# RWKV scan: the joins of the next inverse issued ahead of the scan step, in a PSUM bank of their own, with the inverse and the norms at other places of the step

## The chip, the core and the metric

The kernel runs on one core of a Trainium2 chip. The metric is the device time of one execution in microseconds (us): the median over the runs, each timed from start to end. A profile of one more execution shows each engine by itself: PE (TensorE matmuls; PEld is its weight loads), DVE (VectorE), ACT (ScalarE), POOL (GpSimd) and SP (SyncE, which issues the DMAs). Each engine runs its own list of instructions in the order in which the built program holds them; an instruction whose data or buffer isn't ready holds up those behind it on its engine.

## What is computed

A two-layer backbone over 1024 latent tokens and 256 context tokens of width 1024. Each layer mixes tokens by four groups of heads (mLSTM, Hyena, retention, RWKV-7), projects their outputs together, and ends in a convolutional feed-forward network. The change is in the RWKV group. Its scan, over four heads of 64 channels and in both directions, is

```
def step(s_mem, inp):
    rt, wt, kt, vt, at, bt = inp
    sa = jnp.einsum('bhvk,bhk->bhv', s_mem, at)
    s_new = s_mem * wt[:, :, None, :] + sa[..., None] * bt[:, :, None, :] + vt[..., None] * kt[:, :, None, :]
    return s_new, jnp.einsum('bhvk,bhk->bhv', s_new, rt)
```

followed by `out = g * (head_group_norm(h) + bonus)`. The mLSTM group runs over the same tokens at the same time and shares no data with RWKV until the output projection `y @ w_out`.

## The kernel before

The scan is done in ten steps of 128 tokens, one tile for the forward direction and one for the backward one; each tile holds two chunks of 64 tokens. A step has four parts, each a function:

- `rwkv_prep(s)` loads the step's inputs, makes decays and scaled keys (two gate projections on PE at L496, then ACT and DVE), and forms the 64x64 products of a chunk (`G`, PE at L533) and transposed keys (`bt`, L544). It needs nothing of the scan.
- `rwkv_inverse(s)` inverts the 16x16 diagonal blocks of each chunk's triangular matrix: one DVE transpose into `LM` (L555) and thirty dependent POOL instructions on `XL` (L559, L560).
- `rwkv_tail(s)` joins these blocks into the 64x64 inverse `XT`: two joins (16 to 32, 32 to 64), each of small 32*32 matmuls (L576, L584, L585, L590, L597, L598, L605, L606) with DVE or ACT copies between them. L569 is its first instruction, L611 its last.
- `rwkv_chain(s)` is the scan step itself: for each of two chunks and two directions it multiplies the state (L631, L632), copies (`U`, L634), applies `XT` (L635), copies (`VSA`), and makes the new state (L641, L642, then L644 on DVE); L649 and L650 make the outputs `y`. Step s needs the state of step s-1 and `XT` of step s.

`group_norm` then normalises tiles that both directions have finished (steps 1 and 6 to 9), through a scratch tile `gq`, and stores them (`yw<-gq`).

The PSUM (eight banks) is cut for this stage by `psum(k,cbank=2,ybank=1,pbank=1,dbank=2,mbank=2)`: `cbank` for the scan step and the joins, `pbank` for the gate projections, `dbank` for the products of `rwkv_prep`, `ybank` for outputs, `mbank` for mLSTM and the ada steps.

`layer` starts the scan, issues its first steps, and then `mlstm`, which calls back: 19 side steps in the first layer (17 in the second), each with a share of the modulation matrix (the ada steps, L993) and every second one with a step of the scan. The mLSTM first walks the chunks (states, L753 and L759), then makes ten (eight) tiles of output (L781, L791, L797, L804). The order in which a function is called is only a priority: a scheduler in the build sets each engine's final order from it. After the scan, `load_wo` brings in the output weights (32 loads `wst<-in_w_out`, each split by ACT and DVE at L1035 and L1036), and `mix_out` gathers normalised tiles (`yt<-ym,yh,yr,yw`), transposes them (L1166), splits them (`uh`, L1177) and multiplies (L1042 to L1044). The weights `wo` take memory that the mLSTM held, `yt` takes memory that includes pool `p3` of the scan, and `uh` takes that of the scan's other pools.

Of the kernel before, what the change touches and what calls it, by code (L numbers as in the profile page):

```python
# [10 lines left out]
F32=mybir.dt.float32  # L11
# [418 lines left out]
def rwkv(K,l,pv,last,p1,p2,p3):  # L430


    nc=K.nc; tt=nc.vector.tensor_tensor
    YF=p1.tile([128,10,4,64],F32,name="YF")
    W2=p1.tile([128,512],F32,name="W2"); nc.gpsimd.memset(W2,0.0)
    for i,(w,o) in enumerate((('rwkv_w2','rwkv_w0'),('rwkv_a2','rwkv_a0'))):
        nc.sync.dma_start(W2[i*64:i*64+32].rearrange("p (d c) -> p d c",d=2),K.a[w][l].rearrange("d p c -> p d c"))
        nc.sync.dma_start(W2[i*64+32:i*64+33],K.a[o][l:l+1].rearrange("o d c -> o (d c)"))
    TWA=p1.tile([128,2,2,128],F32,name="TWA"); nc.gpsimd.memset(TWA,0.0)
    rmask=p1.tile([128,2,128],F32,name="rmask"); nc.sync.dma_start(rmask,K.a['c_rwmask'])  # L440
    xl0=p1.tile([128,32,8],F32,name="xl0"); nc.sync.dma_start(xl0,K.a['c_xl0'])
    smask=p1.tile([128,4*65],F32,name="smask"); nc.gpsimd.memset(smask,1.0); nc.gpsimd.memset(smask.rearrange("p (a b) -> p a b",b=65)[:,:,0:1],0.0)
    kas=p1.tile([128,2,2,2],F32,name="kas")
    for a in range(2):
        r=slice(64,128) if a==0 else slice(0,64); o=slice(0,64) if a==0 else slice(64,128)
        nc.gpsimd.memset(kas[o,a],-0.5)
        nc.vector.tensor_scalar(out=kas[r,a,0],in0=pv['ka'][r],scalar1=0.5,scalar2=None,op0=ALU.mult)
        nc.vector.tensor_scalar(out=kas[r,a,1],in0=pv['ka'][r],scalar1=-0.5,scalar2=1.0,op0=ALU.mult,op1=ALU.add)
    AR=[p1.tile([128,2,2,2,2,2,64],F32,name="AR%d"%i) for i in range(3)]
    for t in AR: nc.gpsimd.memset(t[64:128,:,:,:,0],0.0); nc.gpsimd.memset(t[0:64,:,:,:,1],0.0)  # L450
    XT=[p1.tile([128,2,4,128],F32,name="XT%d"%i) for i in range(2)]
    for t in XT: nc.gpsimd.memset(t,0.0)
    I32=p1.tile([128,32],F32,name="I32"); hm=p1.tile([128,2],F32,name="hm"); PI=p1.tile([128,2,4,32],F32,name="PI")
    for i in range(4): nc.scalar.activation(out=I32[i*32:i*32+32],in_=K.ident[i*32:i*32+32,i*32:i*32+32],func=ACTF.Copy)
    for i in range(2): nc.vector.tensor_reduce(out=hm[:,i:i+1],in_=I32[:,i*16:i*16+16],axis=XS,op=ALU.add)
    for i in range(2): nc.scalar.activation(out=PI[:,i],in_=I32.unsqueeze(1).to_broadcast([128,4,32]),func=ACTF.Copy)
    C=dict(AR=AR,XT=XT,I32=I32,hm=hm,PI=PI,YF=YF,W2=W2,TWA=TWA,rmask=rmask,xl0=xl0,smask=smask,kas=kas,p=p2,p3=p3,l=l,pv=pv,last=last,seen=set())
    NS=10
    st=[rwkv_prep(K,C,0)]
    rwkv_inverse(K,C,st[0]); rwkv_tail(K,C,st[0])  # L460
    st.append(rwkv_prep(K,C,1))
    for s in range(NS):
        yield
        if s+1<NS: rwkv_inverse(K,C,st[s+1])
        rwkv_chain(K,C,st[s],st[s+1] if s+1<NS else None,s)
        if s==1 and not last or s>5:
            a,b={1:(8,9),6:(3,4),7:(2,5),8:(1,6),9:(0,7)}[s]
            sl=slice(a,b+1,b-a)
            group_norm(K,YF[:,sl],K.D['yw'].rearrange("(t p) c -> p t c",p=128)[:,sl],2,p2.tile([128,1056],F32,tag="LM",name="gq")[:,0:512].rearrange("p (a t) -> p a t",t=64),"gnw")
        if s+1<NS: rwkv_tail(K,C,st[s+1])  # L470
        if s+2<NS: st.append(rwkv_prep(K,C,s+2))


def rwkv_prep(K,C,s):
    nc=K.nc; act=nc.scalar.activation; tt=nc.vector.tensor_tensor; mm=nc.tensor.matmul; ts=nc.vector.tensor_scalar
    p=C['p']; p3=C['p3']; pv=C['pv']; bank=K.dbank; A=ALU
# [12 lines left out]
    VSA,SV=[X.rearrange("p q d c f e -> p d c q f e") for X in (VSA,SV)]  # L489
    lw=p3.tile([128,8,65],F32,tag="lw",name="lw"); As=p3.tile([128,2,2,128],F32,tag="As",name="As")  # L490
    act(out=lw[:,:,0:1],in_=C['rmask'][:,0,0:1].unsqueeze(1).to_broadcast([128,8,1]),func=ACTF.Copy,scale=0.0)
    bb=[K.pbank(),K.pbank()]
    for i in range(2):
        for d in range(2):
            for ft in range(2):
# [26 lines left out]
    for d in range(2):  # L522
# [8 lines left out]
        for c in range(2):  # L531
            b=bank()
# [8 lines left out]
        b=bank()  # L541
# [21 lines left out]
def rwkv_tail(K,C,P):  # L563
# [5 lines left out]
    for h in range(2): nc.vector.transpose(out=T2[:,4*h:4*h+4].rearrange("p j k d u -> p j (k d u)"),in_=X[:,h*128:h*128+128].rearrange("p (i j) -> p j i",j=4))  # L569
    nc.vector.transpose(out=DT,in_=T2.rearrange("p j k d u -> p (d u) (j k)"))  # L570
    R=[(q,blk,slice(q*64+blk*32,q*64+blk*32+32)) for q in range(2) for blk in range(2)]
    b=K.cbank()
    for d in range(2):
        for u in range(4):
            c,f=u//2,u%2; o=slice(d*64+u*16,d*64+u*16+16)
# [1 line left out]
    for d in range(2):  # L577
        o=slice(d*16,d*16+16)
        nc.vector.scalar_tensor_tensor(out=PI[:,d,:,o],in0=b[:,d*64:d*64+64].rearrange("p (u t) -> p u t",t=16),scalar=C['hm'][:,1-d:2-d],in1=C['I32'][:,o].unsqueeze(1).to_broadcast([128,4,16]),op0=A.mult,op1=A.add)
    b=K.cbank(); Q=p.tile([128,4,32],F32,tag="Q",name="Q"); ZC=p.tile([128,4,32],F32,tag="AX",name="ZC")  # L580
    for u in range(4):
        o=slice(256+u*32,288+u*32)
        for q,blk,r in R:
# [5 lines left out]
            o=slice(d*128+u*32,d*128+u*32+32)  # L589
            for q,blk,r in R: mm(b[r,o],PI[r,d,u],T2[r,:,:,1,u] if d else DT[r,u],start=True,stop=True)  # L590
    for q,blk,r in R: act(out=XT[r,:,:,r],in_=b[r,0:256].rearrange("p (d u t) -> p d u t",d=2,u=4),func=ACTF.Copy)
    b=K.cbank()
    for u in range(4):
        c,f=u//2,u%2; o=slice(u*32,u*32+32)
        for q in range(2):
# [1 line left out]
            mm(b[hi,o],G[lo,0,c,f,q,32:64],ZC[lo,u],start=True,stop=True)  # L597
            mm(b[lo,o],G[hi,1,c,f,q,0:32],ZC[hi,u],start=True,stop=True)  # L598
    act(out=Q.rearrange("p u t -> p (u t)"),in_=b[:,0:128],func=ACTF.Copy)
    b=K.cbank()  # L600
    for u in range(4):
        o=slice(u*32,u*32+32)
        for q in range(2):
# [769 lines left out]
def layer(k,l,out):  # L1373
    nc=k.nc; last=l==1
    D=k.D=k.Ds[l]; k.Dn=k.Ds[l+1] if not last else None
    with ExitStack() as es:
# [19 lines left out]
            with k.tc.tile_pool(name="rt",bufs=1,side="right") as k.p_rt:  # L1396
                retention(k,l,last)
        close_u(k)
        psum(k,cbank=2,ybank=1,pbank=1,dbank=2,mbank=2)
        with ExitStack() as ew:  # L1400
            with ExitStack() as er:
                R=lambda **kw: er.enter_context(k.tc.tile_pool(bufs=1,side="right",**kw))
# [66 lines left out]
```

## Time and profile before

| what | us |
|---|---|
| median of 3 runs | 4250.28 |
| lowest and highest run | 4240.55, 4259.92 |
| the profiled execution, its own time | 4248.15 |
| span of its instructions | 4246.4 |

The RWKV scan and the mLSTM run together twice, once in each layer: from about 767 to 1234 us and from 2942 to 3369 us of the span. The rest (projections, Hyena, retention, feed-forward) isn't touched. Busy time is the time in which an engine had at least one instruction under way; a matmul counts from its start to the end that the profile models, so two matmuls that overlap count once. Times of rows are microseconds from the start of the span, unless marked ns. Two records of PE stand for one fp32 matmul of the program.

### The profile page before, as it was taken

To read this page: it belongs to the slowest core of one execution; us is meant where nothing else is said; L and a number is where in the kernel's file an instruction comes from. 1 tells how busy PE (TensorE), PEld (TensorE's weight loads), DVE (VectorE), ACT (ScalarE), POOL (GpSimd) and SP (SyncE) were. 2 spreads that over 40 slices of the span, in tenths; PEclk is the share of its full clock that TensorE was granted. 3 is DMA by queue.
4 is the path that set the end of the run, shared out by engine and by line. 5 is a ranking of instruction groups with operands and counts; after the bars stand their busy time and mean duration, and the time that the engine had idled before them with its cause. 6 is when DMAs were issued, how large, how long until landed. Compare 5 with 4: busy or idle time off the path is not lost.

```text
span 4246.4 us, 70484 instructions
## 1 busy us (share of the span) xinstructions
PE 3951.2 (93%) x28176; PEld 3225.0 (76%) x28176; DVE 2537.2 (60%) x4756; ACT 1413.6 (33%) x2849; POOL 764.7 (18%) x1538
## 2 busy tenths in 40 slices
PE   5999999799979999999997999997899799999998
PEld 2788887677768888888885678886776678888886
DVE  5755665777669444444448565677767684444447
ACT  4433333554344211111113433344543442212121
POOL 3320023323312000000021221025432220000002
PEclk6999999799989999999998999998898799999999
DMA  4235554344443110111103325554333331111112
GB/s 165 76 96 180 151 156 121 109 149 125 129 147 120 46 40 30 45 40 35 35 30 121 90 87 157 171 162 118 118 115 109 124 111 55 50 40 55 45 50 99
DMA packets 477154, 414.50 MB, mean 98 GB/s; under 512 B 48827, under 2 KB 443284, under 8 KB 474010
## 3 DMA queue, kind: packets, MB, share of 16 engines
q1 hardware_dynamic: 476826, 409.99, 31.1%
q8 instruction: 222, 3.64, 0.3%
q14 instruction: 106, 0.87, 0.1%
HBM read 323.65 MB, written 86.25 MB: 97 GB/s over the span
## 4 chain that ended last, share of the span: by engine, by line
PE 53%; DVE 9%; DMA 4%; issue 2%; ACT 2%; POOL 1%; SPq 1%; DVEq 0%; ACTq 0%; POOLq 0%
PE bank L1043 9%; PE bank L1042 9%; PE bank L1044 9%; PE dbank L1042 6%; PE dbank L1043 6%; PE dbank L1044 6%; DVE bst L1003 1%; DMA xt<-x 1%; DVE facc L1225 1%; PE mbank L993 1%; PE bank L186 1%; DMA adaw<-in_ada_w 1%; PE bank L187 1%; DVE facc L1226 0%; DMA wst<-in_w_out 0%
## 5 line engine op out<-in xcount | busy, mean ns | idle before, releaser
L1042 PE MATMUL dbank<-uh,wh 128*128 128x512 f32 (+1 forms) x2120 | 763.7, 369 | 8.6 <-ACT tmpB L398 5.5
L1043 PE MATMUL dbank<-ul,wh 128*128 128x512 f32 (+1 forms) x2120 | 759.8, 367 | 0.0
L1036 DVE TENSOR_TENSOR wl<-wst,wh 128x1024 fp32r<-128x1024 f32 x146 | 185.9, 1275 | 510.3 <-ACT wh L1035 355.1
L1044 PE MATMUL dbank<-uh,wl 128*128 128x512 f32 (+1 forms) x2120 | 481.5, 367 | 0.0
L1042 PEld LDWEIGHTS dbank<-uh,wh 128*128 128x128 f32 x2120 | 400.6, 189 | 84.0 <-ACT tmpB L398 5.9
L1043 PEld LDWEIGHTS dbank<-ul,wh 128*128 128x128 f32 x2120 | 400.9, 189 | 68.7 <-issue 1.1
L1044 PEld LDWEIGHTS dbank<-uh,wl 128*128 128x128 f32 x2120 | 365.7, 188 | 71.0 <-issue 1.7
L1284 DVE TENSOR_TENSOR facc<-facc,bank 128x512 f32<-128x512 f32 x324 | 221.8, 687 | 205.1 <-PE bank L1044 205.1
L1042 PE MATMUL bank<-uh,wh 128*128 128x512 f32 (+1 forms) x920 | 334.9, 372 | 4.5 <-ACT uh L1030 4.5
L1043 PE MATMUL bank<-ul,wh 128*128 128x512 f32 (+1 forms) x920 | 335.1, 372 | 0.8 <-DVE ul L1031 0.8
L1042 PE MATMUL bank<-wdh,gh 128*128 128x512 f32 x792 | 315.6, 400 | 15.7 <-DVE facc L1298 5.7
L1043 PE MATMUL bank<-wdl,gh 128*128 128x512 f32 x792 | 310.4, 392 | 1.0 <-DVE wdl L1036 1.0
L1253 POOL MEMSET fz<- 128x1 f32 x132 | 7.3, 99 | 1433.4 <-DVE fc L1268 1213.5
L1044 PE MATMUL bank<-wdh,gl 128*128 128x512 f32 x792 | 247.7, 391 | 0.0
L1035 ACT ACTIVATE wh<-wst 128x1024 fp32r<-128x1024 f32 x146 | 154.7, 1060 | 237.5 <-PE dbank L1043 164.5
L1035 ACT ACTIVATE wdh<-wst 128x1024 fp32r<-128x1024 f32 x46 | 48.8, 1062 | 523.7 <-PE bank L1044 431.4
L1044 PE MATMUL bank<-uh,wl 128*128 128x512 f32 (+1 forms) x920 | 211.9, 372 | 0.0
L1042 PEld LDWEIGHTS bank<-uh,wh 128*128 128x128 f32 x920 | 174.1, 190 | 36.1 <-ACT uh L1030 5.6
L1043 PEld LDWEIGHTS bank<-ul,wh 128*128 128x128 f32 x920 | 174.2, 189 | 31.9 <-DVE ul L1031 1.7
L1042 PEld LDWEIGHTS bank<-wdh,gh 128*128 128x128 f32 x792 | 149.7, 189 | 56.9 <-DVE facc L1298 11.0
L1044 PEld LDWEIGHTS bank<-uh,wl 128*128 128x128 f32 x920 | 161.5, 188 | 33.1
L1043 PEld LDWEIGHTS bank<-wdl,gh 128*128 128x128 f32 x792 | 149.7, 189 | 34.6 <-issue 3.2
(490 smaller groups left out, 7856.9 us busy)
## 6 DMA issues: line engine op xcount, KB each, us to landing
wst<-in_ffn_w_up SPq DMA_DIRECT2D x88, 512.0 KB
adaw<-in_ada_w SPq DMA_DIRECT2D x160, 256.0 KB
wst<-in_w_in SPq DMA_DIRECT2D x58, 512.0 KB
wst<-in_ffn_w_down SPq DMA_DIRECT2D x46, 512.0 KB
df<-in_c_F SPq DMA_DIRECT2D x10, 1344.0 KB
xt<-x SPq DMA_DIRECT2D x26, 512.0 KB
df<-in_c_I SPq DMA_DIRECT2D x8, 1344.0 KB
rkk<-wrk SPq DMA_DIRECT2D x10, 1024.0 KB
```

The costliest lines, as they stand in the source:

```text
L186: mm(dst_re,F[:,i],pre(slot),start=True,stop=False); mm(dst_re,F[:,i+1],pim(slot),start=False,stop=True)
L187: mm(dst_im,F[:,i],qim(slot),start=True,stop=False); mm(dst_im,F[:,i+2],qre(slot),start=False,stop=True)
L993: for j in range(2): nc.tensor.matmul(ps[32*j:32*j+2,0:128],k.sc[:,q],w[u][q//2][:,q%2,j*128:j*128+128],start=(q==0),stop=(q==7))
L1003: for h in range(2): nc.vector.bn_stats(out=st[:,h],in_=x[h])
L1035: k.nc.scalar.activation(out=h,in_=st,func=ACTF.Copy)
L1036: k.nc.vector.tensor_tensor(out=lo,in0=st,in1=h,op=ALU.subtract)
L1042: mm(ps,lh,rh,start=(i==0),stop=False)
L1043: mm(ps,lh,rl,start=False,stop=False)
L1044: for i,((lh,ll),(rh,rl)) in enumerate(pairs): mm(ps,ll,rh,start=False,stop=(i==n-1 and more is None))
L1225: for o,i,gg in zip([y[:,h] for h in hs],x,[g[:,h] for h in hs]) if parts else [(y,x,g)]: stt(out=o,in0=i,scalar=m,in1=gg,op0=ALU.subtract ...
L1253: for q in (0,1025,1282): nc.gpsimd.memset(z[:,q:q+1],0.0)
L1284: else: tt(out=d,in0=d,in1=ps,op=ALU.add)
```

## The change

The call of `rwkv_tail` for step s+1 moves ahead of `rwkv_chain` for step s; `rwkv_prep` for step s+2 moves directly behind the scan step, with `rwkv_inverse` for step s+2 right after it (before, that was called at the start of the next round); `group_norm` comes last in the round. The joins take their PSUM from a bank of their own, `tbank`; `pbank` is given up and the gate projections use `dbank`. The scratch tile of the norm moves from the buffer of `LM` (pool `p2`) to that of `As` (pool `p3`).

```diff
-    st.append(rwkv_prep(K,C,1))
+    st.append(rwkv_prep(K,C,1)); rwkv_inverse(K,C,st[1])
     for s in range(NS):
         yield
-        if s+1<NS: rwkv_inverse(K,C,st[s+1])
+        if s+1<NS: rwkv_tail(K,C,st[s+1])
         rwkv_chain(K,C,st[s],st[s+1] if s+1<NS else None,s)
+        if s+2<NS: st.append(rwkv_prep(K,C,s+2)); rwkv_inverse(K,C,st[s+2])
         if s==1 and not last or s>5:
             a,b={1:(8,9),6:(3,4),7:(2,5),8:(1,6),9:(0,7)}[s]
             sl=slice(a,b+1,b-a)
-            group_norm(K,YF[:,sl],K.D['yw'].rearrange("(t p) c -> p t c",p=128)[:,sl],2,p2.tile([128,1056],F32,tag="LM",name="gq")[:,0:512].rearrange("p (a t) -> p a t",t=64),"gnw")
-        if s+1<NS: rwkv_tail(K,C,st[s+1])
-        if s+2<NS: st.append(rwkv_prep(K,C,s+2))
+            group_norm(K,YF[:,sl],K.D['yw'].rearrange("(t p) c -> p t c",p=128)[:,sl],2,p3.tile([128,8,64],F32,tag="As",name="gq"),"gnw")
...
-    bb=[K.pbank(),K.pbank()]
+    bb=[bank(),bank()]
...
-    b=K.cbank()
+    b=K.tbank()
...
-        psum(k,cbank=2,ybank=1,pbank=1,dbank=2,mbank=2)
+        psum(k,cbank=2,tbank=1,ybank=1,dbank=2,mbank=2)
```

The third edit stands at all four places of `rwkv_tail` that take a bank. From `rwkv_prep` on, the changed kernel's line numbers are one lower.

How the instructions stand on PE in the middle of the first layer, at the end of a scan step that the joins for the next one follow (`T` and `DT` are the transposed blocks, `mCS` and `mq` belong to the mLSTM). Before:

```order
L642 MATMUL cbank<-VSA,bt 64x64 x2
L649 MATMUL ybank<-VSA,G 64x64
L650 MATMUL ybank<-SV,AR_6744 64x64 x2
L649 MATMUL ybank<-VSA,G 64x64 x2
L650 MATMUL ybank<-SV,AR_6744 64x64 x2
L649 MATMUL ybank<-VSA,G 64x64 x2
L650 MATMUL ybank<-SV,AR_6744 64x64 x2
L576 MATMUL cbank<-T_11506,G 32x16 x16
L576 MATMUL cbank<-DT,G 32x16 x16
L797 MATMUL mbank<-mCS,mq_10058 128x130 x2
```

The joins begin when the scan step's last output matmul has been issued. In the changed kernel, inside a scan step of the same layer (L589 and L596 are joins, L634, L640 and L641 the scan step, L803 the mLSTM):

```order
L634 MATMUL cbank<-U,XT_6752 128x64 x2
L589 MATMUL tbank<-DT,PI 32x32 x13
L780 MATMUL mbank<-mRU,mVOr 128x512
...
L589 MATMUL tbank<-DT,PI 32x32 x3
L589 MATMUL tbank<-T_10755,PI 32x32 x11
L803 MATMUL mbank<-mV,S 128x65 x4
L589 MATMUL tbank<-T_10755,PI 32x32 x5
L640 MATMUL cbank<-SV,ident 64x64 x2
L641 MATMUL cbank<-VSA,bt 64x64 x2
```

The joins of the next step stand between the scan step's own matmuls, and in shorter pieces. At the end of the second layer, PE has before (L804 is the last mLSTM matmul, the rest of the scan step follows it):

```order
L804 MATMUL mbank<-mV,S 128x65 x4
L635 MATMUL cbank<-U,XT_25742 128x64 x2
L804 MATMUL mbank<-mV,S 128x65 x4
L631 MATMUL cbank<-SV,G 64x64 x2
L632 MATMUL cbank<-SV,AR_25735 64x64 x2
```

Behind these rows come the rest of scan step 8, the joins for step 9, all of scan step 9, and L1042. Now, at the same place:

```order
L631 MATMUL cbank<-SV,AR_25733 64x64 x2
L803 MATMUL mbank<-mV,S 128x65 x8
L634 MATMUL cbank<-U,XT_25743 128x64 x4
L648 MATMUL ybank<-VSA,G 64x64 x2
L649 MATMUL ybank<-SV,AR_25733 64x64 x2
```

Only the last product and the outputs of scan step 9 stand behind the last mLSTM matmul. On SP, at the end of the same layer, before:

```order
L1158 DMA yt<-ym_108 128x2x256
L1158 DMA yt<-yh_109 128x2x256
L1158 DMA yt<-yr_110 128x2x256
L1158 DMA yt<-yw_111 128x2x256
L679 DMA ym_108<-gq 128x2x256
L1060 DMA wst<-in_w_out 128x256 x22
L679 DMA yw_111<-gq 128x2x256
```

and now:

```order
L678 DMA ym_108<-gq 128x2x256
L678 DMA yw_111<-gq 128x2x256
L1059 DMA wst<-in_w_out 128x256 x24
L1157 DMA yt<-ym_108 128x2x256
L1157 DMA yt<-yh_109 128x2x256
L1157 DMA yt<-yr_110 128x2x256
L1157 DMA yt<-yw_111 128x2x256
```

The second layer's first gathers for the output projection stand behind all loads of its weights, where two sets of them stood ahead. In the first layer two sets stand ahead of the 24 loads in both kernels.

## Rows read from the trace of the kernel before

**Rows 1.** The page, busy time of PE.

```profile
PE 3951.2 (93%) x28176; PEld 3225.0 (76%) x28176; DVE 2537.2 (60%) x4756; ACT 1413.6 (33%) x2849; POOL 764.7 (18%) x1538
```

**Rows 2.** Windows: length, busy PE, PEld, DVE, ACT, POOL, clock, DMA share, GB/s.

```profile
850.00:1185.00 335.00, 314.56 (x5462) 239.03 (x5460) 234.90 (x642) 145.64 (x421) 103.76 (x287) 0.95 0.42 132
1185.00:1206.00 21.00, 18.15 (x123) 14.57 (x122) 9.88 (x28) 5.61 (x7) 2.07 (x2) 0.80 0.15 51
3020.00:3312.00 292.00, 268.40 (x4487) 205.40 (x4487) 207.50 (x552) 133.28 (x382) 93.23 (x259) 0.92 0.38 119
3312.00:3361.00 49.00, 34.67 (x608) 29.45 (x606) 29.18 (x84) 20.33 (x62) 8.86 (x24) 0.64 0.31 98
```

**Rows 3.** Timeline (start, us, engine, line), first layer: joins of step 5, scan step 4.

```profile
985.14 0.69 DVE L569 STREAM_TRANSPOSE T<-XL 128x128 f32<-128x128 f32 x2
990.74 0.25 ACT L634 ACTIVATE U<-cbank 128x128 f32<-128x128 f32 x1
1012.78 0.33 PE L650 MATMUL ybank<-SV,AR 128*64 128x64 f32 x3
1029.23 0.26 ACT L634 ACTIVATE U<-cbank 128x128 f32<-128x128 f32 x1
1033.12 0.30 DVE L611 COPY XT<-cbank 32x128 f32<-32x128 f32 x1
```

**Rows 4.** Timeline of PE: matmuls of changing and of equal tile shape (32*32, 64*64).

```profile
845.35 0.19 PE L606 MATMUL cbank<-XT,Q 32*32 32x32 f32 x1
845.47 0.33 PE L631 MATMUL cbank<-SV,G 64*64 64x64 f32 x4
845.73 0.34 PE L632 MATMUL cbank<-SV,AR 128*64 128x64 f32 x4
...
1051.59 0.29 PE L642 MATMUL cbank<-VSA,bt 128*64 128x64 f32 x4
1051.71 0.29 PE L641 MATMUL cbank<-SV,ident 128*64 128x64 f32 x4
```

**Rows 5.** Waits of PE (total, times, longest): 850 to 1185, 3020 to 3312, 760 to 850.

```profile
PE mbank L993 <- DMA adaw<-in_ada_w: 9.9, 11, 3.6
...
PE mbank L993 <- DMA adaw<-in_ada_w: 5.0, 6, 2.0
...
PE pbank L496 <- ACT ex L501: 17.4, 2, 8.8
```

**Rows 6.** Timeline, first layer: from the last mLSTM matmul to the output projection.

```profile
1201.68 3.51 PE L804 MATMUL mbank<-mV,S 128*128 128x65 f32 x16
1212.29 1.09 PE L1166 MATMUL dbank<-ident,yt 128*128 128x128 f32 x4 [2.90 <-DMA yt<-ym]
1217.16 11.84 SPq L1060 DMA_DIRECT2D wst<-in_w_out  x24
1233.58 0.77 PE L1042 MATMUL bank<-wo,uh 128*128 128x512 f32 x1 [20.21 <-ACT uh L1177]
```

**Rows 7.** Timeline, second layer: gather, last mLSTM matmul, last scan output, output projection.

```profile
3265.38 0.37 SPq L1158 DMA_DIRECT2D yt<-ym  x1
3310.24 1.62 PE L804 MATMUL mbank<-mV,S 128*128 128x65 f32 x8
3359.49 0.52 PE L650 MATMUL ybank<-SV,AR 128*64 128x64 f32 x3
3365.73 0.38 SPq L679 DMA_DIRECT2D yw<-gq  x1
3369.09 0.80 PE L1042 MATMUL bank<-wo,uh 128*128 128x512 f32 x1 [4.26 <-ACT uh L1177]
```

**Rows 8.** Tile LM, what its engine waited for; timeline of POOL, one inverse.

```profile
DMA yw<-gq: 6.4, 4
...
993.12 0.27 POOL L559 TENSOR_TENSOR XL<-LM,XL 128x30 f32<-128x30 f32 x1 [3.50 <-DVE LM L555]
1006.83 0.21 POOL L560 TENSOR_TENSOR XL<-XL 128x8 f32<-128x8 f32 x1
```

More of the change, by code (lines that the diff above doesn't have):

```diff
@@ L579, in rwkv_tail @@
         nc.vector.scalar_tensor_tensor(out=PI[:,d,:,o],in0=b[:,d*64:d*64+64].rearrange("p (u t) -> p u t",t=16),scalar=C['hm'][:,1-d:2-d],in1=C['I32'][:,o].unsqueeze(1).to_broadcast([128,4,16]),op0=A.mult,op1=A.add)
-    b=K.cbank(); Q=p.tile([128,4,32],F32,tag="Q",name="Q"); ZC=p.tile([128,4,32],F32,tag="AX",name="ZC")
+    b=K.tbank(); Q=p.tile([128,4,32],F32,tag="Q",name="Q"); ZC=p.tile([128,4,32],F32,tag="AX",name="ZC")
     for u in range(4):
@@ L591, in rwkv_tail @@
     for q,blk,r in R: act(out=XT[r,:,:,r],in_=b[r,0:256].rearrange("p (d u t) -> p d u t",d=2,u=4),func=ACTF.Copy)
-    b=K.cbank()
+    b=K.tbank()
     for u in range(4):
@@ L599, in rwkv_tail @@
     act(out=Q.rearrange("p u t -> p (u t)"),in_=b[:,0:128],func=ACTF.Copy)
-    b=K.cbank()
+    b=K.tbank()
     for u in range(4):
```

## The prediction, made before the changed kernel had run

> **What bounds the kernel now.** I read the page first. PE is busy for 93% of the span [rows 1], so a change that only moves work pays where PE is not full. The two stretches in which the scan runs are then read by windows [rows 2]. While scan and mLSTM run together, PE is busy for 314.56 of 335 us in the first layer (20.4 idle) and for 268.40 of 292 us in the second (23.6 idle). Busy there is not peak: small matmuls overlap, and what looks busy hides short waits. The second layer ends differently: after the last mLSTM matmul, from 3312 to 3361 us, the scan runs alone, with PE busy for 34.67 of 49 us at a clock of 0.64. The first layer ends with the mLSTM alone, from 1185 to 1206 us, with 18.15 of 21 us busy.
>
> Then the timeline of one step in the middle [rows 3]. Scan step 4 runs from its first copy at 990.74 to its last output matmul at 1013.1 us (22 us). The joins of step 5 have their first transpose at 985.14, but their last copy ends only at 1033.4. Scan step 5 had its first product copied at 1029.23 and waits there for that copy. So before the change a round is a scan step (22 us) and the joins (another 16 to 20 us) one after the other, with mLSTM in the gaps. The change takes the joins out of this sequence. Whether that is worth anything depends on whether the gaps were empty, and rows 2 say that they mostly were not.
>
> Last, the two ends. In the first layer the projection (L1042) starts 28.4 us after the last mLSTM matmul (1205.19 to 1233.58): norm, store, 24 loads of weights over 11.84 us and their splits [rows 6]. In the second it starts at 3369.09, 57.2 us after the last mLSTM matmul (3311.86), and it waits there for the scan's last store, issued at 3365.73 [rows 7].
>
> **First layer.** PE's work is the same number of matmuls, but they stand in another order. Rows 4 show what a change of tile shape costs. Four records of 64*64 and then four of 128*64 start 0.26 us apart; groups of four that keep the shape start 0.12 us apart: 0.14 us for a change. From 32*32 to 64*64 the step is 0.12 us where joins follow each other within 0.01 us: 0.11 us. I counted the rows of PE in both built programs whose tile shape differs from the row before, from the first gate projection to the last scan or mLSTM matmul: 486 before, 587 now in the first layer, 435 and 486 in the second. Most of the new ones are at joins cut into pieces, so I take 0.12 us: 101 x 0.12 = +12 us (11 to 14).
>
> Against that, a second stream of ready work covers waits. Of the 20.4 us idle, 9.9 are waits for weights of the ada steps [rows 5], which no order of joins removes. Of the other 10.5 I take half: -5 (0 to -10.5; the hidden waits inside busy time are the first rival). The scan now ends earlier against the mLSTM (32 instead of 16 row-counted L804 matmuls stand behind its last output), so two more tiles run alone, about 21 us (two tiles fill the window from 1185 to 1206 now) at 0.86 busy instead of 0.94 [rows 2]: +2 (0 to +4). The end behind the last mLSTM matmul stays as it is.
>
> **Start of each layer.** The single `pbank` makes the second half of a gate projection wait: 17.4 us in two waits in the first layer [rows 5]. Two `dbank` buffers remove them. Most of it lies ahead of work that waits for memory and DVE anyway; I take -2 for each layer (0 to -8). The price of the bank, that `G` must find both `dbank` buffers free, is nothing: many DVE and ACT instructions lie between the projection's copies and the first product. If that cover were gone, a wait like these 8.8 us would return once a step.
>
> **Second layer, the end.** If the mLSTM still ended at 3311.86, the projection would start 28.4 us later as in the first layer, not 57.2. But the gathers now stand behind the 24 loads. After the last of these come four issues, a landing of some 2.9 us [rows 6], transposes and the split, while in the first layer the gather was ready: +5 (0 to +9). Room: 57.2 - 28.4 - 5 = 24 us.
>
> This room is used up by the work that moves ahead of the last mLSTM matmul: the rest of scan step 8, the joins, and scan step 9 but its end. Alone it keeps PE busy for 34.67 us at clock 0.64, that is 22 us at full clock; 51 more changes of shape add 6. Of the 23.6 us idle in the shared stretch, 5.0 are for ada weights; half of the other 18.6 can be filled, -9 (0 to -18.6). So the mLSTM ends 22 + 6 - 9 = 19 us later (9 to 41). Net -24 + 19 = -5, and -2 for the start.
>
> The other edits cost nothing. The norm's scratch no longer holds `LM`: four waits of 6.4 us in all go [rows 8], inside the stretches already counted. In `As` it is reused only by a projection a whole scan step later; if that cover were gone, a store of some 2 us would return per norm.
>
> **The sum** against the profiled 4248.15 us: first layer +12 - 5 + 2 - 2 = +7, second -24 + 19 - 2 = -7, together 0. **Predicted: 4248 us**, 2 us under the median of the runs shown. These runs lie 19 us apart, so under 0.5%, 21 us, I call no change.
>
> **A rule that speaks against the change.** A change of shape cost 0.11 to 0.14 us in rows 4. The Trainium skill, TensorEngine Tiling (Array Packing), section Key Properties, says that changing the tiling mode drains the TensorE. The trace agrees that a change costs extra, and shows less than a whole matmul. If each new change cost the full 0.19 us of a record [rows 4], the terms would be 19 and 10 instead of 12 and 6: 4259 us, still no change.
>
> **The rivals.** *Cycle, not engine, is the limit (25%).* Rows 3 speak for it: a round is 38 us, of which the scan step is 22. Then the joins are covered completely: all of the 10.5 and 18.6 us is filled, and as much again of hidden waits in the first layer. First layer 12 - 20 + 2 - 2 = -8; second -24 + 9 - 2 = -17, with another 12 us if the moved work also vanishes in hidden waits. That is 4211 us. Against it: rows 2 show 0.94 of the shared stretch busy though a round holds 16 to 20 us of joins, so the mLSTM already filled most of that time; two streams slow each other.
>
> *Joins block the scan (19%, slower).* The joins stand on PE between the scan step's own matmuls. An inverse takes 13.9 us on POOL from 993.12 to 1007.04 [rows 8], which also serves norms and the mLSTM. Before, the joins came a whole scan step after it, and no wait of a join for `XL` showed. Now a late inverse holds the joins' first matmul on PE and everything behind it, both streams. With 2 us in each of 18 steps that is +36: 4284 us. It decides from 1.2 us a step.
>
> *Full drain at every change (6%):* 4259 us, as above.
>
> *The scheduler undoes it:* the place of calls is only a priority. The order excerpts show that the joins did move, so this has no chance of its own.
>
> **Chances.** Forecast, 50%: no change, own range 4231 to 4265 from the bounds of the terms. With the drain rival, and a few per cent of the forecast beyond the edges, no change has 0.53. Faster than 4229 has 0.27 (first rival and the forecast's low edge), slower than 4271 has 0.20 (the blocking joins). The range for 8 in 10 takes in most of both: 4208 to 4282.
>
> **What would show it.** Right: PE at 0.94 to 0.97 busy in the shared stretch; the scan's round shorter, the mLSTM's tile longer; in the second layer L1042 within 33 us or so of the last L804, and at 3355 to 3370 minus the first layer's shift. The shape changes show as a larger sum of busy PE time in the two stretches together. The first rival shows as L804 of the second layer at about 3300 to 3312 less the shift, and the first layer's projection 8 us or more earlier. The second rival shows as PE waits at L575 for `T` or `DT`, tens of us in all. The prediction is wrong if the scan's stretch gets shorter by more than the idle time of rows 2, since then busy PE hid more waits than I allow.

## The result and the profile after

The changed kernel takes 4293.85 us in the median (4289.68 to 4300.24, four runs), the kernel before 4253.66 beside it: ratio 1.0101, interval 1.0078 to 1.0123. It is 40 us slower. 4248 was forecast, with a range from 4208 to 4282.

The page's PE line and span of the changed kernel:

```profile
span 4294.8 us, 70450 instructions
...
PE 3988.3 (93%) x28176; PEld 3241.3 (75%) x28176; DVE 2533.6 (59%) x4756; ACT 1413.0 (33%) x2847; POOL 785.3 (18%) x1538
```

The number of matmuls is the same as in [rows 1], busy PE time is 37 us more. The windows of the changed kernel, in the columns of [rows 2]: first layer shared and mLSTM alone, second layer shared and what follows it.

```profile
850.00:1198.60 348.60, 326.33 (x5378) 246.02 (x5377) 232.74 (x628) 148.46 (x431) 111.56 (x285) 0.94 0.37 115
1198.60:1233.50 34.90, 27.40 (x207) 19.50 (x207) 18.64 (x50) 9.27 (x12) 4.12 (x4) 0.95 0.45 148
3070.00:3387.50 317.50, 292.23 (x4901) 223.35 (x4898) 223.07 (x587) 141.56 (x412) 108.31 (x281) 0.95 0.33 102
3387.50:3422.00 34.50, 8.97 (x72) 7.86 (x72) 21.03 (x55) 19.72 (x46) 2.15 (x3) 0.60 0.55 180
```

Against [rows 2] no idle time was filled: 22.3 us in the first shared stretch (20.4 before), 25.3 in the second (23.6). The ends, in the timeline of PE (first layer's last mLSTM matmuls and first projection; then the second layer's last mLSTM matmuls, the transposes of the late gather, and the projection):

```profile
1231.57 1.90 PE L803 MATMUL mbank<-mV,S 128*128 128x65 f32 x16
1261.77 0.77 PE L1041 MATMUL bank<-wo,uh 128*128 128x512 f32 x1 [21.38 <-ACT uh L1176]
...
3385.38 2.00 PE L803 MATMUL mbank<-mV,S 128*128 128x65 f32 x16
3416.96 3.61 PE L1165 MATMUL dbank<-ident,yt 128*128 128x128 f32 x16 [22.02 <-DMA yt<-ym]
3421.87 0.50 PE L1041 MATMUL bank<-wo,uh 128*128 128x512 f32 x1 [1.31 <-ACT uh L1176]
```

The first layer's mLSTM ends 28.3 us later than in [rows 6], and its projection follows as before, 28.3 us behind it. In the second the projection follows 34.5 us behind, where [rows 7] have 57.2. The losses are therefore two: 28 us in the first layer's scan stretch, and 25 us from the first layer's projection to the second's, net of the 22.7 us saved at its end.

A good part of those 25 us lies ahead of the scan, where no edit was made. Windows of one dense run of products in the second layer's retention (L872, L871; 872, 873 before), from its first product with the state to its last, before and after:

```profile
2906.80:2932.20 25.40, 25.40 (x201) 22.97 (x200) 12.18 (x28) 11.64 (x24) 3.33 (x4) 1.00 0.12 43
```
```profile
2936.40:2982.40 46.00, 45.31 (x200) 41.27 (x200) 11.92 (x27) 11.79 (x24) 5.16 (x6) 0.50 0.04 14
```

The same 200 records take 46.0 us at a granted clock of 0.50 (1.2 GHz), 25.4 at 1.00 (2.4 GHz). In the changed kernel PE idled twice just ahead of it (before, 1.28 us at L422, then 0.31 at L866 and none for `rSS`):

```profile
2927.76 2.72 PE L422 MATMUL dbank<-tmpA,bones 128*128 128x512 f32 x4 [2.59 <-DVE tmpA L418]
...
2936.36 0.69 PE L872 MATMUL bank<-rSS,rT 128*128 128x64 f32 x2 [2.71 <-POOL rSS L846]
```

Last, the gate projections up to 850 us, instructions of their line, before and after:

```profile
L496 PE MATMUL pbank<-TWA,W x80: 272/275/583, 767.4 to 849.6; 128*128 128x128 f32 x80
```
```profile
L495 PE MATMUL dbank<-TWA,W x48: 275/275/422, 767.1 to 835.2; 128*128 128x128 f32 x48
```

In a bank of their own the gate projections had run ahead: five steps (16 records each) against three now.

### The profile page after: what moved, and what is told of

The parts are those of the page before. It is cut to its first block, busy times and chain, and to the rows that moved or that the text cites. A ratio compares the mean times of both kernels' runs of the same rounds, so it can differ in the third digit from the quotient of the medians.

```text
span 4294.8 us, 70450 instructions
## 1 busy us (share of the span) xinstructions
PE 3988.3 (93%) x28176; PEld 3241.3 (75%) x28176; DVE 2533.6 (59%) x4756; ACT 1413.0 (33%) x2847; POOL 785.3 (18%) x1538
## 4 chain that ended last, share of the span: by engine, by line
PE 52%; DVE 9%; DMA 3%; issue 3%; POOL 2%; ACT 2%; SPq 0%; DVEq 0%; ACTq 0%; POOLq 0%
PE bank L1041 9%; PE bank L1042 9%; PE bank L1043 9%; PE dbank L1041 6%; PE dbank L1042 6%; PE dbank L1043 6%; DVE bst L1002 1%; PE dbank L532 1%; DMA xt<-x 1%; DVE facc L1224 1%; PE bank L186 1%; PE bank L187 1%; POOL XL L559 0%; DVE facc L1225 0%; DVE mt L1186 0%
## 5 line engine op out<-in xcount | busy, mean ns | idle before, releaser
L1042 PE MATMUL dbank<-ul,wh 128*128 128x512 f32 (+1 forms) x2120 | 761.0, 368 | 0.0
L1042 PEld LDWEIGHTS dbank<-ul,wh 128*128 128x128 f32 x2120 | 401.5, 189 | 68.8 <-issue 1.1
L1042 PE MATMUL bank<-ul,wh 128*128 128x512 f32 (+1 forms) x920 | 335.2, 372 | 0.8 <-DVE ul L1030 0.8
L1041 PE MATMUL bank<-wdh,gh 128*128 128x512 f32 x792 | 315.9, 401 | 13.6 <-DVE facc L1297 5.9
L1042 PE MATMUL bank<-wdl,gh 128*128 128x512 f32 x792 | 311.0, 393 | 1.3 <-DVE wdl L1035 1.3
L1042 PEld LDWEIGHTS bank<-ul,wh 128*128 128x128 f32 x920 | 174.3, 189 | 31.9 <-DVE ul L1030 1.7
L1080 ACT ACTIVATE z<-dbank 128x512 f32<-128x512 f32 (+1 forms) x160 | 85.6, 536 | 281.2 <-PE dbank L1043 264.4
```

What stands on the lines that cost most here:

```text
L1041: mm(ps,lh,rh,start=(i==0),stop=False)
L1042: mm(ps,lh,rl,start=False,stop=False)
L1080: nc.scalar.activation(out=z[:,oo:oo+n],in_=b[:,:n],func=ACTF.Copy)
```

## The experiments

Each is compared with runs of the kernel before on the same chip (median 4240 to 4245 us). "Stretch" is the time from a layer's first gate projection (767.4 and 2932.7 us before) to its last mLSTM matmul: 437.8 us before and 466.4 after in the first layer, 379.2 and 404.2 in the second. A stretch is read from one profiled execution. The runs are numbered e1 to e15 where their results stand. Five of the traces (the kernel before, e2, e9, e11, e15) have the same order on PE in the first layer, but for a few neighbouring records: their first stretches took 433.1 to 443.7 us, and 12 to 27 us of that was lost to half clock. A difference of 10 us between two stretches is within this scatter.

**One layer at a time.**

```
-psum(k,cbank=2,ybank=1,pbank=1,dbank=2,mbank=2)
+if l==0: psum(k,cbank=2,tbank=1,ybank=1,dbank=2,mbank=2)
+else: psum(k,cbank=2,ybank=1,pbank=1,dbank=2,mbank=2)
...
```

Every other edit of the change stands under the same condition, `l==0` in the first run and `l==1` in the second.

> The change is made in the first layer alone; the second keeps the old order and banks. Theory A (the second layer's retention fell to half clock because the scheduler, working from the first layer's new order, placed the instructions ahead of it otherwise): about +28 us to the end of the first layer's mLSTM, again about +20 us in the retention stage at a granted clock near 0.5, and nothing else: 4253 + 48 = about 4300 us, slower than the whole change or equal to it. Rival B (the retention stage is late because of the second layer's own edits, such as gate projections that must find dbank free): +28 us and the retention at full clock, about 4281 us.

Measured (e1) 1.0077 (1.0053 to 1.0101), 4279 us. The first stretch took 464.9 us. The second layer's retention ran at half clock (45.9 us), although nothing of that layer was changed: theory A, not B. Between the first layer's output projection and the second scan PE's order is that of the whole change, record for record, and differs from before; the wait just ahead of the run is another one, though: 0.88 us for DVE (`tmpB`, L423), none for `rSS`. The total is lower than expected: its old scan stretch took 364.6 instead of 379.2 us, so most of the lost time there was regained; 7 of these 14.6 us are less half clock, and why is not settled.

> The change is made in the second layer alone; the first keeps the old order and banks. Theory A: retention of the second layer at full clock as before (25 us from its first to its last output product), scan and mLSTM end about 25 us later against their start, the output projection starts 24 us sooner behind them: 4253 + 1, within 5 us of no change. Rival B: the retention stage is at half clock here too, and the time is about 20 us longer, 4274 us.

Measured (e2) 0.999 (0.9975 to 1.0005), 4238 us. Retention 25.4 us at full clock; stretch 395.0 us, 15.8 longer than before; projection 35.3 us behind the last mLSTM matmul. Theory A. In this layer alone the change is within 0.3% of neutral.

**Banks without order, order without banks.**

```
-    bb=[K.pbank(),K.pbank()]
+    bb=[bank(),bank()]
-    b=K.cbank()
+    b=K.tbank()
```

The second edit stands at the joins' four places.

> Only the PSUM is cut anew (tbank for the joins, gate projections in dbank); all calls stand in the old order. If the new banks cost by themselves (gate projections and products now compete for dbank), the first layer's mLSTM ends 10 us or more later than 1205 us. If the order of the calls is what costs, it ends within 5 us of 1205, and the total is within 15 us of 4253 unless the retention of the second layer falls to half clock (+20).

Measured (e3) 1.0164 (1.0143 to 1.0184), 4308 us. The first stretch took 483.3 us, the second 417.8: the banks alone cost more than the whole change.

```
-        if s+1<NS: rwkv_inverse(K,C,st[s+1])
+        if s+1<NS: rwkv_tail(K,C,st[s+1])
         rwkv_chain(K,C,st[s],st[s+1] if s+1<NS else None,s)
+        if s+2<NS: st.append(rwkv_prep(K,C,s+2)); rwkv_inverse(K,C,st[s+2])
```

> Only the order of the calls is new (joins ahead of the scan step, preparation and inverse behind it); joins stay in cbank with the scan step, gate projections in pbank, the norm's scratch in LM. If the order costs, the first layer's mLSTM ends 25 us or more later than 1205 us: the joins then also wait for the scan step's own buffers, so more than with the bank of their own. If it was the banks, it ends near 1205. Total 4253 + 28 or more, plus 20 if the retention falls to half clock.

Measured (e4) 1.0058 (1.0043 to 1.0073), 4268 us; first stretch 460.8 us, second 373.1. Order costs too, but less, and in another way (the table below). "The order alone" and "the banks alone" both fall; the two losses don't add up (23 and 45.5 against 28.6 together).

**Which bank.** Gate projections in dbank, one bank left unused:

> Old order, joins in cbank as before; only the gate projections move from pbank to dbank, and the eighth bank is left unused. The built program has 512 changes of tile shape in the first layer's scan stretch (486 before, 593 with the joins in a bank of their own) and 49 unbroken runs of joins (46 before, 98). Theory A (the joins' own bank lets the scheduler cut them into pieces between the scan step's matmuls, and that costs): from the first gate projection to the last mLSTM matmul 440 us or less above half-clock differences (437.8 before, 483.3 with both banks new). Rival C (the gate projections take dbank from the products and that costs): 465 us or more.

Measured (e5) 1.0038 (1.0016 to 1.006), 4269 us; first stretch 451.4 us: between the two theories. The second layer's retention run took 40.4 us here, part of it at half clock. Then the spare bank as a third one for joins and scan step together, in the old order and in the new:

```
-psum(k,cbank=2,ybank=1,pbank=1,dbank=2,mbank=2)
+psum(k,cbank=3,ybank=1,dbank=2,mbank=2)
```

> Old order, gate projections in dbank; the eighth bank goes to cbank (three, shared by joins and scan step) in place of a bank for the joins alone. 560 changes of shape, 80 runs of joins in the first layer. Theory A: any bank that lets joins and scan step lie side by side cuts the joins, so most of the loss returns: 460 to 475 us from the first gate projection to the last mLSTM matmul of the first layer. If only a single bank reserved for the joins hurts (each join waits for the read of the one before), it is near 440.

Measured (e6) 1.0151 (1.011 to 1.0193), 4321 us, stretch 483.6: as bad as the reserved bank, 9 us worse than expected. In the old order a third bank for joins and scan step costs some 32 us in the first stretch, reserved or shared. That it costs because it cuts the joins isn't shown: the table below has fewer changes of shape here than with the reserved bank, and more waits.

> The whole change, but joins take their PSUM from cbank, which gets the eighth bank (three). 511 changes of shape and 67 runs of joins in the first layer (587 and 83 with the bank of their own). Theory A: 76 changes fewer at 0.12 us are 9 us, fewer waits another 5: about 450 us from the first gate projection to the last mLSTM matmul of the first layer instead of 466, total some 15 to 25 us under the changed kernel. If the order costs and not the banks, it stays at 466.

Measured (e7) 1.0102 (1.0062 to 1.0143), 4297 us, stretch 473.6. There are fewer changes of shape, and no time was won: a miss of theory A.

**The price of a change of shape.** First by itself:

```
+for a,b in ((S32,S64),(S32,S128),(S64,S128)):
+    for _ in range(48): M(*a)
+    for _ in range(48): M(*b)
+    for _ in range(48): M(*a); M(*b)
```

> The kernel before with matmuls added at its start that nothing uses: for each of three pairs of shapes (32x32 with 64x64, 32x32 with 128x64, 64x64 with 128x64) 48 of the one, 48 of the other, then the two in turn, 48 times. Cost of a change of shape: interval in turn less the mean of the two intervals in a row. The prediction's value: 0.11 to 0.14 us at full clock (twice that at half). A full drain: 0.19 us or more at full clock.

The granted clock fell to half in the middle (windows of that kernel, e8):

```profile
64.00:105.00 41.00, 41.00 (x299) 33.23 (x298) 0.00 (x0) 0.00 (x0) 0.00 (x0) 0.50 0.00 1
105.00:112.00 7.00, 7.00 (x90) 6.16 (x88) 0.00 (x0) 0.00 (x0) 0.00 (x0) 0.98 0.01 2
```

The trace holds no granted clock ahead of 57.5 us, where windows print 1.00; that the records there ran at half is read from their pace: 64x64 in a row start 107 ns apart there and in the half-clock window alike, and 128x64 start 108 ns apart up to 57 us and 58 behind it. At the half-clock pace two records of one shape start 53.6 ns (32x32), 107.2 (64x64) and 108.2 (128x64) apart; in turn the mean is 159.6, 161.7 and 201.4 ns a record, with a change every second record. A change costs 2 x (159.6 - 80.4) = 158 ns, 162 and 187 ns. In the short full-clock parts it is 107 and 127 ns a record in turn, and 58.3 for 128x64 in a row; with half of 53.6 and 107.2 for the other two shapes (an estimate, they have no row at full clock), a change costs 0.13 and 0.14 us. The forecast's 0.11 to 0.14 holds, a full drain (0.19) does not. At half clock a change costs 0.16 to 0.19, not twice as much. The added matmuls also altered the order of the rest, and the first stretch took 471.5 us in this one run.

Then in place, in the scan step of the kernel before, 76 matmuls that nothing reads (the control has `K.ident[:,0:64]`, 64 rows of output):

```
                     for r,q in HQ: mm(b2[r,f*64:f*64+64],bt[:,d,ch,f,q],...)
+                    if C['l']==0: mm(b[0:32,384:416],K.ident[0:32,0:32],K.ident[0:32,0:32],start=True,stop=True)
```

> The kernel before with 76 more matmuls in the first layer's scan step, 32x32, on unused columns of the scan step's own bank, whose result nothing reads: 630 changes of tile shape in the stretch instead of 486. Theory A (a change costs about 0.18 us of PE time in place): PE's time at full clock without waits grows by 144 x 0.18 = 26 us plus some 4 us for the matmuls themselves (310.7 to about 340). The prediction's price of 0.12: 21 us. If changes are hidden and the growth came from elsewhere: under 8 us.

> The same 76 matmuls in the same place, but 128x64 like their neighbours: 469 changes of shape. Theory A: PE's time at full clock without waits grows by 76 x 2 records x 0.06 = 9 us less 17 changes at 0.18 (3 us): 6 us; it is some 25 us less than with the foreign shape. If the matmuls and not the shapes cost, both are alike.

Foreign shape (e13): 1.0129 (1.0105 to 1.0154), 4295 us; same shape (e14): 1.0036 (1.002 to 1.0052), 4255 us. PE's own time ("pace" and "small" of the table below) grew by 15.1 and 3.3 us. The price in place is then about 0.08 us, not 0.18: 143 more changes in the window, and 76 matmuls of two records each, which took 3.3 us in the same shape and some 4 us by the expectation, so 11 to 12 us for 143 changes. The theory as put there falls: matmuls that moved past the start of the window ("pace") had gone into its 0.18. But the first stretch took 486.5 against 442.3 us, and the windows say where (foreign, then same):

```profile
850.00:1253.50 403.50, 376.12 (x5728) 281.14 (x5727) 243.86 (x667) 153.37 (x428) 105.28 (x288) 0.88 0.36 112
```
```profile
846.00:1205.80 359.80, 334.65 (x5731) 258.21 (x5730) 246.01 (x666) 148.37 (x426) 105.42 (x288) 0.95 0.41 125
```

The same count of records, and a clock of 0.88 instead of 0.95: 31 of the 44 us are time at half clock. The profiled executions lie 62 us apart, the medians 40; the rest of the 62 is mostly the second layer's retention, which took 46.6 us with the foreign shape and 25.4 with the same one.

**The wait ahead of the retention.** The kernel before with 3.7 us more on POOL:

```
     for t in XT: nc.gpsimd.memset(t,0.0)
+    if l:
+        for t in XT: nc.gpsimd.memset(t,0.0); nc.gpsimd.memset(t,0.0)
```

> The kernel before with four more memsets of XT (0.92 us each) on POOL at the start of the second layer's scan, which stand between the retention's state updates (rSS). PE's order up to the scan is unchanged. Theory A (a wait of PE for a late rSS in front of or inside the retention's dense run of products lets the granted clock fall to half, and it stays there): the 3.7 us on POOL turn the run from 25.4 us at full clock into 40 to 46 us at half. Rival D (PE's order in that stage makes the difference, not the wait): 25.4 us plus at most 3.7.

Measured (e9) 1.0043 (1.0026 to 1.0061), 4267 us. PE's wait and the run behind it:

```profile
2908.85 0.69 PE L875 MATMUL bank<-rSS,rT 128*128 128x64 f32 x2 [2.46 <-POOL rSS L849]
```
```profile
2908.80:2955.80 47.00, 46.95 (x200) 42.51 (x200) 11.75 (x27) 11.69 (x24) 5.18 (x6) 0.50 0.05 17
```

PE's order from the first layer's projection to the second scan is the same as before, a wait of 2.46 us is new, and the run takes 47.0 us at half clock. Rival D falls: late work on POOL, without another order on PE, does it. The wait 9 us earlier (L422, for `tmpA`) grew too, from 1.28 to 2.59 us as in the changed kernel, so that the wait for `rSS` alone is enough isn't shown.

```
+    ar=nc.vector if l else nc.gpsimd
-    for t in AR: nc.gpsimd.memset(...)
+    for t in AR: ar.memset(...)
```

> The changed kernel with the six memsets of AR (6.4 us) of the second layer moved from POOL to DVE, so that rSS is ready earlier. Theory A: PE no longer waits 2.7 us for rSS, the retention's dense run takes 25 us instead of 46.3 at full clock; total some 10 to 21 us below the changed kernel's 4294 (the scan's start is partly bound by loads that go on meanwhile). Rival D: the run stays above 40 us.

Measured (e10) 1.0081 (1.0059 to 1.0104), 4284 us, against 1.0101 for the change. The run still took 42.0 us, but it doesn't tell the theories apart: with the memsets on DVE, PE now waited 8.6 us (ending 11 us ahead of the run), still 1.1 us for `rSS` at its start, and 1.0 us inside it. That the run would be fast in the changed kernel without these waits was therefore not tested.

**Parts in one layer or alone.** First the new order (as in the run with the order alone) in the second layer only:

```
+        if s+1<NS and l==1: rwkv_tail(K,C,st[s+1])
         rwkv_chain(K,C,st[s],st[s+1] if s+1<NS else None,s)
+        if s+2<NS and l==1: st.append(rwkv_prep(K,C,s+2)); rwkv_inverse(K,C,st[s+2])
```

> Only the order of the calls is new, and only in the second layer; all banks and the norm's scratch are old. PE's order is that of before up to the end of the first layer's output, and in the second scan stretch that of the run with the new order in both layers, which took 424.9 us from the first gate projection to the output projection (436.4 before). So 11 us below the kernel before (4241 to 4245 in these comparisons): 0.3% faster, if what decides is order and banks; if the first layer's history matters, no change.

Measured (e11) 1.0 (0.9985 to 1.0016), 4246 us. The second layer did what was expected (425.6 us to the projection); in the profiled execution the first layer, with its unchanged order on PE, took 5.9 us more in its stretch, 8.2 us more of it lost to half clock, which is within the scatter named above. No gain shows. Then only the joins moved, in both layers:

```
         if s+1<NS: rwkv_inverse(K,C,st[s+1])
+        if s+1<NS: rwkv_tail(K,C,st[s+1])
         rwkv_chain(K,C,st[s],st[s+1] if s+1<NS else None,s)
-        if s+1<NS: rwkv_tail(K,C,st[s+1])
```

> Only the joins move ahead of the scan step, in both layers; inverse, preparation, banks and norm as before. 456 changes of tile shape in the first layer (486 before, 587 in the change). Over the eight scan stretches measured so far PE's time without waits, at full clock, grew by 0.18 us for each change of shape: that makes this one about 5 us less than before (310.7). The rest (waits, half clock) is open: 25 to 45 us of waits, 19 to 41 us of lost clock. Total within 30 us of before; if the ahead-moved joins themselves cost, PE's own time is 325 us or more.

Measured (e12) 1.0155 (1.0127 to 1.0183), 4315 us, slower than the 30 us allowed. PE's longest wait of the joins from 850 us to the projection (total, times, longest):

```profile
PE cbank L576 <- DVE T L569: 10.3, 2, 9.6
```

Without the early inverse the scan falls back (last output at 1270.8 us, the last mLSTM matmul at 1207.1), and the mLSTM no longer covers it. The long wait for the inverse ends at 1234.0 us, behind the mLSTM: it follows from the falling back and isn't shown to be its cause. Last, the second layer's new order together with the norm's new scratch there:

```
-            group_norm(...,p2.tile([128,1056],F32,tag="LM",name="gq")...,"gnw")
+            group_norm(...,p3.tile([128,8,64],F32,tag="As",name="gq") if l==1 else ...,"gnw")
```

> The new order of calls and the norm's scratch in As, in the second layer alone; all banks old. 433 changes of shape there (435 before, 486 in the change). The order alone took 52 us from the last mLSTM matmul to the output projection and 373.5 us up to it; with the scan keeping up with the mLSTM as in the change that wait would be 35 us. If the moved work costs less than it frees: 5 to 10 us below the kernel before. If it only trades one for the other, as the runs before suggest: no change.

Measured (e15) 1.0083 (1.0066 to 1.01), 4277 us, 31 us above the run with the order alone in that layer. The scan ended 65 us behind the mLSTM, and the projection came 83.7 us behind it. The trace shows where: the last inverse starts on POOL at 3322.4 us, behind a wait of 25.0 us for an mLSTM value (`dn`, L812), against 3292.7 with the order alone. Why the norm's scratch in As brings that order here, and what it does in the change, was not followed up. No version beats the kernel before.

## Why the prediction was wrong

Two steps failed. The larger: the sum has no term for anything outside the two scan stretches, and the second layer's retention took 20.6 us more. The other: the cover of idle time in the first layer, put at -5 us, was not there. The first layer's +7 became +28.

The first stretch of the runs, worked out from the traces. It starts 83 us behind the first gate projection. From each interval between the starts of two following PE records, half of the time at half clock is taken off; "pace" is what the records would take at the usual interval of their kind in the kernel before, "small" the excess up to 0.35 us (changes of shape and whatever else is as short), "waits" the excess of the longer ones, "half clock" what was taken off (us). Another choice of the usual interval moves the growth from before to the change: "pace" to 3 to 7 us, "small" to 11 to 17, "waits" to 5 to 9. So the columns are good to a few us.

```
run                 changes  length  pace  small  waits  half clock
before                  459   354.8  184.2  126.5   25.1   19.1
change                  554   383.4  190.3  137.6   33.8   22.2
first layer only (e1)   552   381.9  189.1  137.5   33.7   22.2
banks only (e3)         560   400.3  190.1  139.6   36.8   34.2
order only (e4)         478   377.8  184.4  124.8   30.9   37.8
gates in dbank (e5)     481   368.4  189.7  125.8   26.7   26.8
cbank 3, old (e6)       527   400.6  188.8  131.6   46.3   34.1
cbank 3, new (e7)       486   390.6  188.7  127.5   35.6   39.3
```

**Shape changes: right in size.** The term was +12; "small" grew by 11.1 us for 95 more changes, 0.117 us each. The price alone was 0.13 to 0.14, in place 0.08. One price for every change isn't shown: with the order alone and the gates alone 19 and 22 more changes added nothing (-1.7 and -0.7 us). What the prediction didn't see is who makes them: the bank, not the order. Order alone has 19 more changes, banks alone 101.

**Gate projections: the sign was wrong.** The term was -2 for each layer, since dbank removes the waits at L496. These waits went, but so did the running ahead: 48 instead of 80 records by 850 us (the rows above). "Pace" is up by 4.5 to 6.1 us in each of the six runs of the table with the gates in dbank, and by 0.2 in the one without: work that had lain in the start now stands in the full stretch. Moving the gates alone cost 13.6 us in the window; 7.7 of it is half clock, no more than the scatter of one order.

**Cover: the step that failed in the first layer.** "Of the other 10.5 I take half: -5 (0 to -10.5)". PE's idle time in the shared stretch rose instead, from 20.4 to 22.3 us, and PE was busy for 0.936 of it (0.94 to 0.97 was to show that the forecast is right). In sum the second stream filled nothing; these are the longest waits of the changed kernel there:

```profile
PE mbank L992 <- DMA adaw<-in_ada_w: 9.3, 10, 2.1
PE tbank L604 <- ACT Q L598: 1.7, 1, 1.7
PE mbank L960 <- DMA adaw<-in_ada_w: 1.4, 1, 1.4
PE mbank L796 <- DVE S L791: 1.2, 1, 1.2
```

Of the 8.7 us by which "waits" grew, about half lies behind the scan's last output, where the mLSTM runs alone. The prediction let that part add +2 (0 to +4); it took 34.9 us instead of 21, with 7.5 us idle instead of 2.9, most of it waits for the weights of the ada steps (before, then now):

```profile
PE mbank L993 <- DMA adaw<-in_ada_w: 2.1, 2, 1.6
PE mbank L992 <- DMA adaw<-in_ada_w: 5.8, 3, 3.6
```

The bounds for the shared stretch allowed no loss at all, though the prediction had PE waits of the joins for a late inverse as its second rival. Why the idle time stayed, with a second stream at hand, isn't shown.

**First layer in all:** +7 forecast, +28.3 measured. In the window: pace 6.1, small 11.1, waits 8.7, half clock 3.1, less 0.4 for rounding and the records at its edges: 28.6.

**Second layer: its terms hold as far as one trace can tell, and what was missing is the retention.** With the change there alone the mLSTM ended 15.8 us later against the scan's start (forecast 19) and the projection came 21.9 us sooner behind it (room 24, with the late gather inside it): 6 us less in all, where -24 + 19 = -5 was forecast. That is partly luck: 7 us of it are less half clock, and in e9, with PE's order of before in that stretch but for a few records, the same part was 7.5 us shorter too. In the full change the mLSTM ended 25.0 us later and the projection came 22.7 sooner.

The retention took 20.6 us more, at half clock. The prediction had counted everything outside the two scan stretches as untouched, and this step is the larger failure. The first layer's edits bring it about (it is there with the change in that layer alone, and not with the change in the second alone): PE's order between the two scans differs with them, and PE waited just ahead of the run, 2.71 us for rSS in the whole change and 0.88 us for tmpB with the first layer alone. That such delays suffice without another order is shown by the late memsets on POOL; which of the waits decides is open. Those memsets cost 18 us by the ratio (1.0043) and 24 by the medians (4267 against 4242); in their profiled execution the stretch behind took 8 us less.

The three parts, 28.3 and 24.6 us to the two projections and 4.4 us less behind the second, make the 48.4 us between the two profiled spans; the medians lie 40 us apart.

**The norm's scratch** was put at nothing. With the old banks, in the second layer, it cost 31 us (4277 against 4246); what it costs with the new banks no run separates.

**The rivals.** The joins that block the scan gave nearly the measured time (4284) by a mechanism that the trace doesn't show: PE's waits for T or DT at L575 are 0.9 us in the first shared window and 1.3 in the second. That it came near 4294 is chance. That the cycle is the limit falls: with the joins off its path the scan's last output came 431.5 us behind the first gate projection, 417.6 before, so the scan of the first layer didn't get shorter; in the second it did, by 20 us (427.3 to 406.9), and the mLSTM ended 25.0 us later for it. The full drain falls with 0.08 to 0.14 us for a change. The Trainium skill, TensorEngine Tiling (Array Packing), section Key Properties, says that a change of tiling mode drains the TensorE: the runs agree that a change costs time, and put it below the length of one of these matmuls.

What stays open: why a run loses more or less to half clock in the first scan stretch (12 to 48 us over all runs, not in step with the number of changes: 38 with 478, 22 with 554). The order plays a part (three traces with the change's order in that layer lost 22.2, 22.2 and 23.9 us), but one order can bring 12 to 27. It is the largest term in several runs, and can't be read from the built program. No run separates the norm's scratch from the order and the banks in the first layer.

## What to carry to other kernels

A bank of its own need not remove waits: here it let the scheduler cut the joins into more pieces, and the bank given up for it had let another stream run ahead. Count shape changes and what has run ahead in the built program, before crediting cover to a queue that is already 94% full. And where a scheduler orders the whole program, an edit in one stage moves others: look for runs of dense matmuls behind short waits, where some 1 to 3 us of idle time went with 20 us lost (e1, e9 and the change).

## What the runs showed of the hardware

- A wait of PE of 2.46 us ahead of a dense run of matmuls (and one 9 us earlier that grew from 1.28 to 2.59 us) went with a fall to half clock that lasted for the whole run, 47 us at 100% busy; with 0.31 us the clock was full throughout (e9 against before, same order on PE). Eight more runs without a wait above 0.31 us at the start or inside took 25.4 us. With 0.84 us at the start the clock stayed full (e12), with 0.88 and 0.92 it fell for the whole run (e1, e13), with 1.12 for 3.4 us only, and again behind a wait of 1.03 us inside (e10); with 1.81 us inside it fell 1.1 and 1.5 us behind the end of the wait (e5, e7). The length of the one wait doesn't decide alone.
- In the first scan stretch PE lost 12 to 48 us to half clock while it was busy for 89 to 94% of it. Of the five traces with one order in that layer two (before, e9) fell at the same places, 150, 263 and 365 us behind the first gate projection, two more near these (e2 at 157, 262 and 365, e15 at 150, 266 and 369), and one elsewhere (e11).
- 76 matmuls of 32x32 among 128x64 ones cost 40 us in the medians (4295 against 4255) and 62 in the profiled executions. Of the 62 some 12 are PE's own time, 31 half clock in the first stretch and 21 half clock in the retention; small gains and losses elsewhere nearly cancel.
